# An Lp pooling kernel: all stores from the queue of the loads, in place of a queue of their own

## The chip, the cores and the metric

The kernel runs on one core of a Trainium2 chip. A core has a matrix engine, TensorE (not used here), VectorE (DVE in the profile), ScalarE (ACT), GpSimd (POOL), the SyncE queue (SP) and sixteen DMA engines, which move data between the device memory (HBM, here "dram") and the on-chip memory (SBUF, 128 partitions). A DMA is issued by one of the engines: the profile names the issuing queue SPq or ACTq. The metric is the device time of one execution in microseconds (us). Before the change it is 395.04 us, the median of three runs (394.88 to 395.09).

## The reference

The input is 32 x 256 x 4096 float32, 134.22 MB; the output 32 x 256 x 1024, 33.55 MB. With p = 2 and windows of 4 that don't overlap, each output is the root of the mean of four squares.

```python
batch, channels, length = 32, 256, 4096
kernel_size, p = 4, 2.0
for i in range(length // kernel_size):
    window = np.abs(x[:, :, 4 * i:4 * i + 4]) ** p
    result[:, :, i] = np.mean(window, axis=-1) ** (1.0 / p)
```

Windows lie one after another in memory, so the kernel treats x as one flat row of numbers and cuts it as it likes, in multiples of four.

## The kernel before

The flat input is cut into **groups**. A group's block of x is spread over 128 partitions, so that each partition reads one unbroken run, and its results are one block of the output. Nine groups have two loads each, then one has three and one has one. A load goes into a **slot**; there are three slots' worth of input buffers (52.7 KB per partition each) and two result buffers. The first 18 loads fill a slot each; the last four share two slots.

```python
W, O_W = 13184, 6592
X_SLOTS, O_SLOTS = 3, 2
slots = [[(W, [4416, 4384, 4384])]] * 18
slots += [[(6592, [3296, 3296])] * 2, [(6592, [3296, 3296]), (5056, [2528, 2528])]]
groups = [2] * 9 + [3, 1]
late = {7, 8, 9, 10}     # groups whose results are stored at the very end
in_x = {9, 10}           # groups whose results lie in a free input slot
```

Loads are issued from SP, two slots ahead of the work; the next one is issued as soon as a slot has been summed. Each load is worked in chunks of about 4400 columns: ScalarE squares in place, VectorE sums by fours into the result tile, and ScalarE then takes the root of a quarter of the sum, in place. The root of a chunk is put behind the square of the next chunk, so that ScalarE needn't wait for VectorE.

```python
def load(i):
    ...
    nc.sync.dma_start(out=v, in_=block(xf, g, 1)[:, src:src + w])

stored = {}

def store(g, queue, until=None):
    first = stored.get(g, 0)
    until = columns[g] // k if until is None else until
    queue.dma_start(out=block(of, g, k)[:, first:until], in_=ots[g][:, first:until])
    stored[g] = until

def root(g, o, ends):
    nc.scalar.activation(out=o, in_=o, func=Act.Sqrt, scale=1.0 / k)
    if ends and g not in late:
        store(g, nc.scalar)
    elif g == 0 and g not in stored:
        store(g, nc.scalar, o.shape[1])
...
pending = None
for i in range(n):
    s, _, w, chunks = loads[i]
    while ahead < n and loads[ahead][0] < s + X_SLOTS:
        load(ahead)
        ahead += 1
    ...
    for step in chunks:
        v = xs[i][:, c:c + step]
        nc.scalar.activation(out=v, in_=v, func=Act.Square)
        o = ots[g][:, at + c // k:at + (c + step) // k]
        nc.vector.tensor_reduce(out=o, in_=v.rearrange("p (n j) -> p n j", j=k), ...)
        if pending is not None:
            root(*pending)
        c += step
        pending = (g, o, i == firsts[g] + groups[g] - 1 and c == w)
root(*pending)
for g in sorted(late):
    store(g, nc.sync)
```

Stores go out of two queues. Groups 0 to 6 are stored from the ScalarE queue, right behind the root that ends the group; group 0 in two parts, its first chunk at once and the rest when the group ends. Groups 7 to 10 are stored from SP, after all loads.

Of the kernel before, what the change touches and what calls it, by code (L numbers as in the profile page):

```python
# [1 line left out]

# [4 lines left out]


@with_exitstack
def kernel(  # L10
    ctx: ExitStack,
    tc: tile.TileContext,
    x: bass.AP,
    p: float,
    kernel_size: int,
    out: bass.AP,
):

    nc = tc.nc

    assert float(p) == 2.0, "kernel specialized for p == 2"
    k = int(kernel_size)
    assert k == 4, "kernel specialized for kernel_size == 4"

    P = nc.NUM_PARTITIONS
    fp32 = mybir.dt.float32
    Act = mybir.ActivationFunctionType
    xf = x.rearrange("b c l -> (b c l)")
    of = out.rearrange("b c l -> (b c l)")
    total = xf.shape[0] // P
# [5 lines that stand above are left out]
    groups = [2] * 9 + [3, 1]  # L42
    late = {7, 8, 9, 10}
    in_x = {9, 10}


    loads = [(s, sum(w for w, _ in slot[:j]), *slot[j]) for s, slot in enumerate(slots)
             for j in range(len(slot))]
    n = len(loads)
    assert sum(w for _, _, w, _ in loads) == total  # L50

    firsts = [sum(groups[:g]) for g in range(len(groups))]
    assert sum(groups) == n
    group_of = [g for g, count in enumerate(groups) for _ in range(count)]
    columns = [sum(w for _, _, w, _ in loads[firsts[g]:firsts[g] + groups[g]])
               for g in range(len(groups))]

    x_pool = ctx.enter_context(tc.tile_pool(name="x_pool", bufs=X_SLOTS))
    o_pool = ctx.enter_context(tc.tile_pool(name="o_pool", bufs=O_SLOTS))
    ctx.enter_context(tc.manual_schedule())  # L60

    def block(flat, g, div):
        at, width = sum(columns[:g]) * P // div, columns[g] * P // div
        return flat[at:at + width].rearrange("(p w) -> p w", p=P)

    slot_tiles = {}
    xs = {}

    def load(i):
        s, at, w, _ = loads[i]  # L70
        if at == 0:
            slot_tiles[s] = x_pool.tile([P, W], fp32, name="xt")
        v = slot_tiles[s][:, at:at + w]
        g = group_of[i]
        src = sum(loads[j][2] for j in range(firsts[g], i))
        nc.sync.dma_start(out=v, in_=block(xf, g, 1)[:, src:src + w])  # L76
        xs[i] = v

    ots = {}

    stored = {}

    def store(g, queue, until=None):
        first = stored.get(g, 0)
        until = columns[g] // k if until is None else until
        queue.dma_start(out=block(of, g, k)[:, first:until], in_=ots[g][:, first:until])  # L86
        stored[g] = until

    def root(g, o, ends):
        nc.scalar.activation(out=o, in_=o, func=Act.Sqrt, scale=1.0 / k)  # L90
        if ends and g not in late:
            store(g, nc.scalar)
        elif g == 0 and g not in stored:
            store(g, nc.scalar, o.shape[1])

    ahead = 0
    while ahead < n and loads[ahead][0] < X_SLOTS - 1:
        load(ahead)
        ahead += 1
    pending = None  # L100
    for i in range(n):
        s, _, w, chunks = loads[i]
        while ahead < n and loads[ahead][0] < s + X_SLOTS:
            load(ahead)
            ahead += 1
        g = group_of[i]
        if i == firsts[g]:
            pool, width = (o_pool, O_W) if g not in in_x else (x_pool, W)
            t = pool.tile([P, width], fp32, name="ot" if g not in in_x else "xt")
            ots[g] = t[:, 0:columns[g] // k]  # L110
        at = sum(loads[j][2] for j in range(firsts[g], i)) // k
        assert sum(chunks) == w
        c = 0
        for step in chunks:
            v = xs[i][:, c:c + step]
            nc.scalar.activation(out=v, in_=v, func=Act.Square)  # L116
            o = ots[g][:, at + c // k:at + (c + step) // k]
            nc.vector.tensor_reduce(  # L118
                out=o, in_=v.rearrange("p (n j) -> p n j", j=k),
                axis=mybir.AxisListType.X, op=mybir.AluOpType.add,  # L120
            )
            if pending is not None:
                root(*pending)
            c += step
            pending = (g, o, i == firsts[g] + groups[g] - 1 and c == w)
    root(*pending)
    for g in sorted(late):
        store(g, nc.sync)


# [1 line left out]
_INS = ['x', 'p', 'kernel_size']  # L132
_OUTS = [((32, 256, 1024), 'float32')]

_NUMBERS = {'p': 2.0, 'kernel_size': 4}


# [26 lines left out]
```

## Time and profile before

| | before |
|---|---|
| time, median of 3 | 395.04 us |
| span of the profiled execution | 393.3 us |
| VectorE busy | 282.4 us, 72% |
| ScalarE busy | 292.7 us, 74% |
| bytes moved by DMA | 167.79 MB, mean 427 GB/s |
| a full load (6592 KB), issue to landing | 39.7 us |
| a store of a full group (3296 KB) from the ScalarE queue, issue to landing | 27.1 us |
| square of 4384 columns, ScalarE | 3845 ns |
| sum of 4384 columns by fours, VectorE | 4720 ns |
| root of 1096 columns, ScalarE | 1105 ns |

The profile gives the busy time of each engine, the same in forty equal slices of the span, the DMA queues with their bytes and their share of sixteen engines' time, the chain of work that ended last, and groups of instructions with what they waited for. L90 is the line of the root, L116 that of the square, L118 that of the sum; L76 issues the loads and L86 the stores. In a line such as `[4.84 <-DMA xt<-in_x_dram]` the bracket is the engine's idle time before the instruction, and what ended it. A DMA's time to landing counts from its issue, so it holds the time behind other transfers of its queue as well.

### The profile page before, as it was taken

Reading aid. Unit: us, or ns where it says so; the run is one execution under the profiler, and the core shown is the slowest. Engines: PE = TensorE matmul, PEld = TensorE weight load, DVE = VectorE, ACT = ScalarE, POOL = GpSimd, SP = SyncE. Lnnn points to the kernel's source line nnn. Section 1 sums busy time; section 2 is a strip of 40 time slices with the busy share of each in tenths; the row PEclk is TensorE's granted clock in tenths of the full one; section 3 lists DMA queues with packets and bytes.
Section 4 is the critical chain, followed back from the end, with each engine's and each line's share of the span. In section 5 each row is a group of like instructions: output and inputs, shape, how many; then the busy total and the mean of one; then the engine's idle time right before and its main releaser. Section 6 shows DMA issues by size and latency. Waiting matters only on the chain.

```text
span 393.3 us, 318 instructions
## 1 busy us (share of the span) xinstructions
DVE 282.4 (72%) x62; ACT 292.7 (74%) x126; POOL 0.2 (0%) x4
## 2 busy tenths in 40 slices
DVE  0068979595959495949594959495859586899992
ACT  1098978687776778686868685859595959899991
POOL 0000000000000000000000000000000000000000
DMA  8999998999999999999999999999999999999997
GB/s 343 429 429 447 453 434 366 472 397 434 421 464 424 461 434 400 464 434 430 394 464 426 432 432 432 426 429 442 429 425 434 461 451 429 400 429 428 436 424 304
DMA packets 4898, 167.79 MB, mean 427 GB/s; under 512 B 544, under 2 KB 544, under 8 KB 800
## 3 DMA queue, kind: packets, MB, share of 16 engines
q1 hardware_dynamic: 3744, 144.15, 85.1%
q10 hardware_dynamic: 1152, 23.63, 14.0%
q14 instruction: 2, 0.02, 0.0%
HBM read 134.22 MB, written 33.55 MB: 427 GB/s over the span
## 4 chain that ended last, share of the span: by engine, by line
DMA 58%; ACT 21%; DVE 16%; issue 2%; another core or an unknown queue 1%; ACTq 0%; SPq 0%
DMA xt<-in_x_dram 58%; ACT xt L116 17%; DVE ot L118 12%; DVE xt L118 3%; ACT ot L90 3%; ACT xt L90 1%; ACTq L86 0%; SPq L76 0%; ACTq L116 0%
## 5 line engine op out<-in xcount | busy, mean ns | idle before, releaser
L118 DVE TENSOR_REDUCE ot<-xt 128x1096 f32<-128x4384 f32 (+1 forms) x54 | 255.4, 4731 | 102.9 <-ACT xt L116 102.6
L116 ACT ACTIVATE xt<-xt 128x4384 f32<-128x4384 f32 (+3 forms) x62 | 230.5, 3718 | 89.2 <-DMA xt<-in_x_dram 85.9
L90 ACT ACTIVATE ot<-ot 128x1096 f32<-128x1096 f32 (+1 forms) x54 | 59.9, 1109 | 1.8 <-DVE ot L118 0.9
L118 DVE TENSOR_REDUCE xt<-xt 128x824 f32<-128x3296 f32 (+1 forms) x8 | 27.0, 3385 | 1.3 <-ACT xt L116 1.2
L90 ACT ACTIVATE xt<-xt 128x824 f32<-128x824 f32 (+1 forms) x8 | 6.8, 844 | 3.0 <-DVE xt L118 2.9
L116 ACT ACT_TABLE_LOAD x1 | 1.3, 1283 | 0.7 <-PEq L145 0.7
L90 ACT ACT_TABLE_LOAD x1 | 1.3, 1283 | 0.0
L145 POOL MEMSET const-bfloat16-1.0<- 128x1 bf16 x1 | 0.1, 103 | 0.0
L145 POOL MEMSET const-uint8-127<- 128x1 uint8 x1 | 0.1, 103 | 0.0
L145 POOL MEMSET const-float32-1.0<- 128x1 f32 x1 | 0.1, 100 | 0.0
L145 POOL MEMSET const-float32-0.0<- 128x1 f32 x1 | 0.1, 99 | 0.2 <-issue 0.2
## 6 DMA issues: line engine op xcount, KB each, us to landing
xt<-in_x_dram SPq DMA_DIRECT2D x18, 6592.0 KB, 39.7
out_dram<-ot ACTq DMA_DIRECT2D x6, 3296.0 KB, 27.1
xt<-in_x_dram SPq DMA_DIRECT2D x3, 3296.0 KB, 24.4
out_dram<-ot SPq DMA_DIRECT2D x2, 3296.0 KB, 29.6
out_dram<-ot ACTq DMA_DIRECT2D x1, 2744.0 KB, 27.4
xt<-in_x_dram SPq DMA_DIRECT2D x1, 2528.0 KB, 26.3
out_dram<-xt SPq DMA_DIRECT2D x1, 2472.0 KB, 9.3
out_dram<-xt SPq DMA_DIRECT2D x1, 632.0 KB, 5.0
```

The lines of the kernel that those rows point to most:

```text
L90: nc.scalar.activation(out=o, in_=o, func=Act.Sqrt, scale=1.0 / k)
L116: nc.scalar.activation(out=v, in_=v, func=Act.Square)
L118: nc.vector.tensor_reduce(out=o, in_=v.rearrange("p (n j) -> p n j", j=k), axis=mybir.AxisListType.X, op=mybir.AluOpType.add,)
L145: nc = _bacc.Bacc("TRN2", target_bir_lowering=False, num_devices=1)
```

## The change

All stores are issued from SP, in turn with the loads, and none from ScalarE. The store of a group is still issued where its last root is: behind the first sum of the next group's first load. In SP's order it stands behind the load that was issued ahead for that step, and ahead of the next one. Group 0 is stored in one piece. The aim is one queue in which transfers run in a chosen order, with a ScalarE that issues nothing.

The bookkeeping of pending roots is rewritten as a list, with two numbers, FINE = 0 (from which load on a chunk gets a root of its own) and LAG = 1 (how many chunks later the root comes).

```diff
+    FINE, LAG = 0, 1
...
-    stored = {}
-
-    def store(g, queue, until=None):
-        first = stored.get(g, 0)
-        until = columns[g] // k if until is None else until
-        queue.dma_start(out=block(of, g, k)[:, first:until], in_=ots[g][:, first:until])
-        stored[g] = until
+    def store(g, queue):
+        queue.dma_start(out=block(of, g, k), in_=ots[g])
 
     def root(g, o, ends):
         nc.scalar.activation(out=o, in_=o, func=Act.Sqrt, scale=1.0 / k)
         if ends and g not in late:
-            store(g, nc.scalar)
-        elif g == 0 and g not in stored:
-            store(g, nc.scalar, o.shape[1])
+            store(g, nc.sync)
...
-    pending = None
+    pending = []
+    done = 0
     for i in range(n):
...
-            if pending is not None:
-                root(*pending)
+            total_sum(ots[g][:, summed:summed + step // k], v, i)
+            while pending and pending[0][0] <= done - LAG:
+                root(*pending.pop(0)[1:])
+            done += 1
             c += step
-            pending = (g, o, i == firsts[g] + groups[g] - 1 and c == w)
-    root(*pending)
+            summed += step // k
+            ends = summed == columns[g] // k
+            if ends or i >= FINE:
+                pending.append((done - 1, g, ots[g][:, rooted:summed], ends))
+                rooted = summed
+    for job in pending:
+        root(*job[1:])
     for g in sorted(late):
         store(g, nc.sync)
```

More of the change, by code (lines that the diff above doesn't have):

```diff
@@ L91, in root, with total_sum @@
         if ends and g not in late:
-            store(g, nc.scalar)
-        elif g == 0 and g not in stored:
-            store(g, nc.scalar, o.shape[1])
+            store(g, nc.sync)
+    def total_sum(o, v, i):
+        nc.vector.tensor_reduce(
+            out=o, in_=v.rearrange("p (n j) -> p n j", j=k),
+            axis=mybir.AxisListType.X, op=mybir.AluOpType.add,
+        )
     ahead = 0
@@ L110 @@
             ots[g] = t[:, 0:columns[g] // k]
-        at = sum(loads[j][2] for j in range(firsts[g], i)) // k
+            summed = rooted = 0
         assert sum(chunks) == w
@@ L116 @@
             nc.scalar.activation(out=v, in_=v, func=Act.Square)
[L117 to L121, printed above, removed]
-            if pending is not None:
-                root(*pending)
-            c += step
-            pending = (g, o, i == firsts[g] + groups[g] - 1 and c == w)
-    root(*pending)
+            total_sum(ots[g][:, summed:summed + step // k], v, i)
+            while pending and pending[0][0] <= done - LAG:
+                root(*pending.pop(0)[1:])
+            done += 1
+            c += step
+            summed += step // k
[5 more added lines that the diff above has]
+        root(*job[1:])
     for g in sorted(late):
```

## The prediction
> **What bounds the kernel now.** I read the page first: the DMA row of the forty slices, then the queues, then the chain.
>
> ```profile
> DMA  8999998999999999999999999999999999999997
> q1 hardware_dynamic: 3744, 144.15, 85.1%
> q10 hardware_dynamic: 1152, 23.63, 14.0%
> HBM read 134.22 MB, written 33.55 MB: 427 GB/s over the span
> DMA 58%; ACT 21%; DVE 16%; issue 2%; another core or an unknown queue 1%; ACTq 0%; SPq 0%
> ```
>
> The sixteen DMA engines are never free between the first slice and the last. The shares of the two queues add to 99.1% of sixteen engines' span, so 0.9% of 393.3 us, 3.5 us, is all the DMA time that stands empty, start and end included. Nothing that only moves bytes about can win more than that. The two queues also give a price per byte: q1 (all loads and the last four stores) 144.15 MB in 0.851 x 393.3 = 334.7 us, 430.7 GB/s; q10 (stores alone) 23.63 MB in 0.140 x 393.3 = 55.1 us, 429 GB/s, and that share is rounded by a third of a per cent. A stored byte costs what a loaded byte costs.
>
> Next the beats of the loop, in the timeline of ScalarE: the first square of a slot starts when its load has landed.
>
> ```profile
> 285.43 3.88 ACT L116 ACTIVATE xt<-xt 128x4416 f32<-128x4416 f32 x1 [4.84 <-DMA xt<-in_x_dram]
> 304.93 3.88 ACT L116 ACTIVATE xt<-xt 128x4416 f32<-128x4416 f32 x1 [4.43 <-DMA xt<-in_x_dram]
> 324.34 3.88 ACT L116 ACTIVATE xt<-xt 128x4416 f32<-128x4416 f32 x1 [4.83 <-DMA xt<-in_x_dram]
> 339.98 3.88 ACT L116 ACTIVATE xt<-xt 128x4416 f32<-128x4416 f32 x1 [1.05 <-DMA xt<-in_x_dram]
> ```
>
> A load is 128 x 13184 x 4 B = 6.750 MB, a store of a full group half of it, 3.375 MB. With a store beside them two loads take 324.34 - 285.43 = 38.91 us: 16.875 MB at 433.7 GB/s. The last full load has no store beside it and takes 15.64 us: 431.6 GB/s. Each time ScalarE idles 4.4 to 4.8 us for the load: compute has slack in every slot.
>
> Last, the stretch table, for what the engines do in one such beat, in the unmixed load, and at the end of the kernel where all loads are in and only stores run.
>
> ```profile
> 285.43:324.34 38.91, 28.38 (x6) 29.14 (x12) 0.00 (x0) 1.00 1.00 433
> 324.34:340.00 15.66, 11.52 (x3) 14.54 (x7) 0.00 (x0) 1.00 0.98 426
> 340.00:369.40 29.40, 27.49 (x7) 28.36 (x13) 0.00 (x0) 1.00 1.00 430
> 369.40:377.30 7.90, 7.51 (x4) 7.87 (x6) 0.00 (x0) 1.00 1.02 441
> 377.30:385.10 7.80, 7.34 (x3) 6.46 (x5) 0.00 (x0) 1.00 0.95 411
> ```
>
> Columns are VectorE busy, ScalarE busy, GpSimd, the clock, the DMA share and GB/s. VectorE and ScalarE work 28.4 and 29.1 us of a 38.9 us beat. The GB/s of short stretches swing because a long packet is counted where it falls; landings are surer. The last load is issued at 343.1 us and lands after 26.3 us, at 369.4; the two stores that follow are issued at 343.56 and 359.5 and land after 33.7 and 25.5 us, at 377.3 and 385.0. That is 15.6 us for 6.750 MB, **stores alone** at 432 GB/s, 7.8 us each, out of one queue in which loads went before.
>
> [...] 38.91 us for two loads and a store is what 2 x 15.64 + 7.8 = 39.1 us makes one after the other. [...]
>
> **The change, part by part.** Call the loads L0 to L21, the stores S0 to S10, S6 the last that is not late.
>
> *Removed.* Eight issues of 0.34 us on ScalarE, with some 0.41 us of idle time shown after each. ScalarE has 4.4 to 4.8 us free in every slot, so this is worth 0 on the path. One of eight stores goes (552 KB early, 2744 KB later, become one of 3296 KB): no bytes.
>
> *Unchanged.* The lists with FINE = 0 and LAG = 1 give the old order: each root still follows the square and the sum of the next chunk. All arithmetic and the four late stores stay.
>
> *Moved.* In program order the SP queue is L0 L1 L2 L3 L4 S0 L5 L6 S1 L7 L8 S2 and so on. S(g) waits for a root that ends one square and one root (3.9 + 1.1 us) after a load's landing; the load behind it waits for three sums of that slot, and now SP waits up to 19.1 us for those in any case (309.4 us in 17 waits, by the view of its own waits). So no load is issued later because of the store ahead of it.
>
> *Where the store now runs.* It no longer shares turns with a load but runs whole, after the load issued before it. From the durations above: L0 lands at 19.6, L1 at 35.5, L2 at 51.2, L3 at 66.8, L4 at 82.5, S0 at 90.3, L5 at 106, L6 at 121.6, S1 at 129.4. [...]
>
> *Does the queue stay filled?* L5 needs slot 2: L2 lands at 51.2, plus a square of 3.9 and three sums of 4.73 = 14.2, is 69.4 us; the queue then has work until 90.3. L6 needs slot 0 again: 66.8 + 18.1 = 84.9, with work until 106. Some 21 us are in hand each time.
>
> *The result buffer.* Group g+2 writes into the buffer of group g. S0 lands 7.8 us after L4, the first load of group 2. VectorE could start 3.9 us after that landing and now must wait some 3.9 us more; the same for groups 3 to 8, seven times, 27 us in all. Within the slot: sums from 90.3 to 90.3 + 14.2 = 104.6, and L5 lands only at 106. Slot 1 is free at 104.6, its next load is issued then, and the queue holds work until 129.4. So the wait costs slack and not time.
>
> *The sum.* Landing of L17: 19.57 + 15.94 (L1 as measured) + 16 x 15.64 + 7 x 7.8 = 340.4 us, against 339.98. The tail after it is the same bytes in the same queue and the same chain of squares, sums and roots, 52.4 us to the last landing. **+0.4 us** on 395.04: 395.4.
>
> **The rivals.** *The buffer wait gets on the path.* For it: the wait is real, and the slot that suffers it ends only 1.4 us ahead of the next load. If all 27 us showed, the time would be 422. Against: to delay a load the 21 us in hand in the queue must be used up first, and a beat has 38.9 us for 29.1 of ScalarE work.
>
> *A turn between reading and writing costs time.* The tail shows one change from loads to stores without loss (7.9 us for the first store), but the old trace never shows one queue go from a store back to a load. Seven such joints at 0.3 us each would be 2.1 us: 397.5. Mixed traffic at 433.7 against 431.6 alone leans that way; over the 131.6 MB of L2 to L17 and seven stores the difference is 1.5 us, which gives 396.5.
>
> *One queue is better.* Loads no longer lose turns to stores, so each arrives sooner after its issue. For it: ScalarE is freed. Against: the bytes ahead of L17 are the same, and no more than 3.5 us are empty now, most of it at the start, where L0 takes 19.57 us in place of 15.6. I give it 0.5 us: 394.5.
>
> **Range and chances.** The centre is 395.4 us. The low end, 394.0, is the third rival with a little more than I give it; the high end, 397.6, is the second. 2% is 7.9 us. A gain of that size is more than the empty DMA time, so 0.01. A loss of it needs the buffer wait to empty the queue, or joints of over 1 us each: 0.02. Within 2%: 0.97.
>
> **What would show the steps right or wrong.** Right: DMA shares adding to 98.5% or more, all in q1; two loads and a store still 38.8 to 39.3 us, but uneven, some 15.6 to the group's first load and 23.4 to its second; stores landing some 42 us after issue in place of 27; VectorE waiting for the store of the result, seven times, some 25 to 30 us in all; SP waits for the roots with the loads' own wait shortened by as much. Wrong: an empty stretch in the DMA row at each store, ScalarE's idle time for loads growing by far more than the seven waits, or a load whose time from issue to landing is under 16 us, which would mean that the queue had run dry.

## The result, and the profile after

The changed kernel takes 397.11 us, the median of six runs (396.80 to 397.23); before took 394.92 us in six runs beside them (394.78 to 395.09). The ratio is 1.0055, 95% interval 1.0042 to 1.0068: within 2%, but slower, by 2.2 us at the medians. The spans of the two profiled executions are 395.3 and 393.3 us.

On the page of the changed kernel, the DMA row, the one queue that is left, the chain and the issues of the stores and full loads (in this kernel L85 is the root, L90 the sum and L116 the square):

```profile
DMA  8999999989999999999999999999999999999996
q1 hardware_dynamic: 4752, 167.77, 98.8%
DMA 67%; ACT 15%; DVE 15%; issue 0%; SPq 0%; DVEq 0%; ACTq 0%
xt<-in_x_dram SPq DMA_DIRECT2D x18, 6592.0 KB, 37.4
out_dram<-ot SPq DMA_DIRECT2D x9, 3296.0 KB, 41.8
```

The queue never ran dry: there is no empty slice, the share is 98.8%, and a load has 37.4 us from issue to landing, far above the 15.6 us of its own transfer. A store now waits behind loads and lands after 41.8 us in place of 27.1. In the packets' records of before, the 128 rows of each of S1 to S6 are spread over 20.9 to 21.8 us, with 96 to 98 whole rows of loads in that time; here they lie within 10.4 to 11.3 us, with 14 or 15. The chain holds more DMA than before, 67% for 58%, as it now runs through the stores as well, with 21% of the span.

The view of the waits shows what was moved. First two lines of before, where L90 is the root and L118 the sum, then the changed kernel:

```profile
ACT xt L116 <- DMA xt<-in_x_dram: 85.9, 18, 17.6
ACT ot L90 <- DVE ot L118: 0.9, 1, 0.9
...
DVE ot L90 <- ACT xt L116: 67.0, 29, 23.6
ACT xt L116 <- DMA xt<-in_x_dram: 64.4, 18, 17.7
DVE ot L90 <- DMA out_dram<-ot: 38.7, 7, 6.6
ACT ot L85 <- DVE ot L90: 28.9, 8, 4.0
```

VectorE waits seven times for the result buffer, 38.7 us in all. That is all of its idle time ahead of those seven sums, and some of it is a wait for the load and its square. The first of the seven sums:

```profile
91.51 9.38 DVE L90 TENSOR_REDUCE ot<-xt 128x1104 f32<-128x4416 f32 x2 [6.65 <-DMA out_dram<-ot]
```

Its square ends at 83.68 + 3.88 = 87.56 us (the line is below), so the store alone holds it up for 3.95 us; over the seven it is 27.8 us. ScalarE's wait for loads fell from 85.9 to 64.4 us, and its wait for VectorE rose from 0.9 to 28.9: idle time changed its name.

The loss is in the landings, in ScalarE's timeline. The rows are the first squares of L2, L3, L4, L5, L6, then of L10, L11, L12, and of L17:

```profile
50.85 3.88 ACT L116 ACTIVATE xt<-xt 128x4416 f32<-128x4416 f32 x1 [1.01 <-DMA xt<-in_x_dram]
66.53 3.89 ACT L116 ACTIVATE xt<-xt 128x4416 f32<-128x4416 f32 x1 [1.10 <-DMA xt<-in_x_dram]
83.68 3.88 ACT L116 ACTIVATE xt<-xt 128x4416 f32<-128x4416 f32 x1 [2.57 <-DMA xt<-in_x_dram]
107.00 3.88 ACT L116 ACTIVATE xt<-xt 128x4416 f32<-128x4416 f32 x1 [4.82 <-DMA xt<-in_x_dram]
123.15 3.88 ACT L116 ACTIVATE xt<-xt 128x4416 f32<-128x4416 f32 x1 [1.56 <-DMA xt<-in_x_dram]
...
201.47 3.88 ACT L116 ACTIVATE xt<-xt 128x4416 f32<-128x4416 f32 x1 [0.99 <-DMA xt<-in_x_dram]
224.82 3.88 ACT L116 ACTIVATE xt<-xt 128x4416 f32<-128x4416 f32 x1 [4.83 <-DMA xt<-in_x_dram]
240.40 3.88 ACT L116 ACTIVATE xt<-xt 128x4416 f32<-128x4416 f32 x1 [1.00 <-DMA xt<-in_x_dram]
...
342.07 3.88 ACT L116 ACTIVATE xt<-xt 128x4416 f32<-128x4416 f32 x1 [4.85 <-DMA xt<-in_x_dram]
```

The uneven beat is there: 23.35 us from L10 to L11 (a store lies between) and 15.58 to L12, 38.93 in all, as good as before. But L4, **the load right ahead of the first store**, takes 83.68 - 66.53 = 17.15 us, 1.5 more than L3, and L6, ahead of the second, 16.15. L17 starts at 342.07 us, against 339.98 before. The stretch table has the same by its rate in the last column:

```profile
50.85:66.53 15.68, 14.28 (x4) 14.52 (x6) 0.00 (x0) 1.00 1.00 431
66.53:83.68 17.15, 15.66 (x4) 14.52 (x6) 0.00 (x0) 1.00 1.01 409
83.68:123.15 39.47, 27.30 (x7) 29.03 (x13) 0.00 (x0) 1.00 1.00 431
201.47:240.40 38.93, 28.29 (x7) 29.03 (x12) 0.00 (x0) 1.00 1.00 432
```

409 GB/s at a DMA share of 1.01: the engines are busy all the time, but some packets take longer. The trace keeps every packet. A row, one partition's part of a load, is one packet of 52.7 KB; it takes an engine 1.947 us at the median in both kernels, a row of a full store 0.978 us. Below, from the packets' own records, are the times by which packets after 22 us were over the median of their size (those over by more than 0.05 us), summed over the sixteen engines; the part of them between 95 us and the end of L17, without the two rows in each run that stand beside a fetch of instructions; and the times at which engines ended, by their own landings:

```
            late time   first cluster of late packets   late time    L4 and S0 in,   L17, first    L17, last
            engine-us   (us of the span: engine-us)     after 95 us  last engine     engine ends   engine ends
before        12.8      30-51: 2.9;  59-65: 8.5             0.0         90.79          338.28        339.89
after         25.6      78-80: 16.6                         7.4         91.39          338.64        341.99
all_act       14.4      43-50: 2.0;  54-61: 11.4            0.1         89.93          338.30        339.52
s0_only_sp    17.9      78-79: 15.2                         1.0         90.42          338.29        339.85
s0_act        27.4      57-63: 18.8                         7.6         90.48          338.63        340.82
early_sp      19.9      47-49: 15.0                         4.0         91.38          338.38        341.42
twice         34.8      76-79: 17.1                        13.3         91.06          339.06        342.19
turns14       25.7      76-79: 18.4                         4.1           -            339.61        342.33
cut_before    25.3      78-81: 18.1                         5.7         91.11          338.90        341.59
no_inline      1.0      none                                0.0           -            283.17        284.34
```

(All but the first two are experiments, below; each line is one profiled execution.) In the changed kernel all sixteen engines are late at 78 to 80 us, about 1.0 us each, with their last row of L4, the one right ahead of S0 (one engine with the row before it too). Small clusters of 0.9 to 2.6 engine-us lie at 119, 157, 236, 275 and 315 us, one ahead of each of S1, S2, S4, S5 and S6, on four to ten engines each. At L17 the quickest engine is only 0.36 us later than before, and the slowest 2.1 us. ScalarE starts on L17 at 342.07 us, behind the slowest engine, so that is the loss.

In these two executions the first store is the lesser part of it. When L4 and S0 are both in, the slowest engine is 0.6 us behind before (91.39 against 90.79); the other 1.5 us come over the six later stores. Before has late packets at its first store too, 11.4 engine-us in its two parts. What it has none of is late time after 95 us.

### The profile page after: what moved, and what is told of

Same layout as the page of the kernel before. It is cut to its first block, busy times and chain, and to the rows that moved or that the text cites. A ratio compares the mean times of both kernels' runs of the same rounds, so it can differ in the third digit from the quotient of the medians.

```text
span 395.3 us, 330 instructions
## 1 busy us (share of the span) xinstructions
DVE 281.7 (71%) x62; ACT 291.8 (74%) x126; POOL 0.2 (0%) x4
## 3 DMA queue, kind: packets, MB, share of 16 engines
q1 hardware_dynamic: 4752, 167.77, 98.8%
## 4 chain that ended last, share of the span: by engine, by line
DMA 67%; ACT 15%; DVE 15%; issue 0%; SPq 0%; DVEq 0%; ACTq 0%
DMA xt<-in_x_dram 46%; DMA out_dram<-ot 21%; ACT xt L116 12%; DVE ot L90 12%; DVE xt L90 3%; ACT ot L85 2%; ACT xt L85 1%; SPq L76 0%; DVEq L90 0%; ACTq L116 0%
## 5 line engine op out<-in xcount | busy, mean ns | idle before, releaser
L90 DVE TENSOR_REDUCE ot<-xt 128x1096 f32<-128x4384 f32 (+1 forms) x54 | 254.7, 4729 | 105.7 <-ACT xt L116 67.0
L116 ACT ACTIVATE xt<-xt 128x4384 f32<-128x4384 f32 (+3 forms) x62 | 230.3, 3716 | 64.4 <-DMA xt<-in_x_dram 64.4
L85 ACT ACTIVATE ot<-ot 128x1096 f32<-128x1096 f32 (+1 forms) x54 | 59.9, 1110 | 29.6 <-DVE ot L90 28.9
L90 DVE TENSOR_REDUCE xt<-xt 128x824 f32<-128x3296 f32 (+1 forms) x8 | 27.0, 3384 | 1.3 <-ACT xt L116 1.2
L85 ACT ACTIVATE xt<-xt 128x824 f32<-128x824 f32 (+1 forms) x8 | 6.7, 843 | 3.0 <-DVE xt L90 2.9
## 6 DMA issues: line engine op xcount, KB each, us to landing
xt<-in_x_dram SPq DMA_DIRECT2D x18, 6592.0 KB, 37.4
out_dram<-ot SPq DMA_DIRECT2D x9, 3296.0 KB, 41.8
```

## The experiments

A **ring** here means the row of transfers of one queue. Theory **J**: a joint from a load to a store in one ring delays the load's last packets. Rivals: **E**, the early store of the first chunk was what before gained from; **B**, VectorE's wait for the result buffer costs the time. P and F, later, divide J.

**all_act**: the stores go back to ScalarE's queue, but whole.

```diff
         if ends and g not in late:
-            store(g, nc.sync)
+            store(g, nc.scalar)
```

> The changed kernel with the seven inline stores, each whole, on the ScalarE queue: against before it lacks only the early store of the first chunk. Theory J (each joint from a load to a store in one ring costs time on some DMA engines, and none joins when the stores have a ring of their own): 394.9 to 395.4 us, last waits of VectorE for a store gone. Theory E (the early first chunk of before was what saved the time): 396.5 us or more. Theory B (VectorE's wait for the result buffer is what costs): as J, 395, since a shared turn lands the store early.

Measured: 394.73 us against 394.79 of before, a ratio of 0.9999 (0.9991 to 1.0008), 0.2 us under J's figure. E falls: the early part of group 0 is worth nothing, and the rewritten lists cost nothing. The queue is the whole change.

**s0_only_sp** and **s0_act**: the first store on one queue, the other six on the other.

```diff
-            store(g, nc.sync)
+            store(g, nc.sync if g == 0 else nc.scalar)     # s0_only_sp
+            store(g, nc.scalar if g == 0 else nc.sync)     # s0_act
```

> S0 alone on the SP queue, S1 to S6 on the ScalarE queue. Theory J with a dear first joint (in the changed kernel's trace all sixteen DMA engines are about 1 us late there, against about 0.45 us in the trace of before): 395.3 to 395.9 us, that is about 0.4 to 0.8 of the 2.2 us. Theory J with equal joints, and theory B (one of seven waits): 395.2 us, a seventh of 2.2 us above before.

> S0 on the ScalarE queue, S1 to S6 on SP. Theory J with a dear first joint: 396.3 to 396.7 us. Equal joints, or theory B: 396.8 us, six sevenths of 2.2 us above before.

Measured: 396.01 us for S0 alone on SP, 1.0028 of before (1.0021 to 1.0035), and 396.57 us for the six others, 1.0043 (1.0029 to 1.0057), against 394.79 of before. By the times, S0 alone brings 1.2 us, more than J with a dear first joint gave it, and the six others 1.8; the interval of the six holds the figures of both forms of J. That the two add to 3.0 and not to 2.2 is not explained.

The traces do not bear out a dear first joint in the ring. In s0_act the first store in the ring of the loads is S1, and no row ahead of it is late. The sixteen engines are late at S0 instead, 18.8 engine-us, though S0 has the ScalarE queue to itself. In these runs, what makes all the engines late goes with the first store of the kernel, in whichever queue. Its size varies: all_act does the same work in the same queues up to S1 and has 13.4 engine-us there. And in s0_only_sp the profiled execution, the quickest of a wide scatter (394.97 to 396.50), has the late rows at S0, 15.2 engine-us, with L4 at 16.69 us, and is still as quick as before; what made the others slower is in no trace.

The later stores set the runs apart. With S1 to S6 on the ScalarE queue (before, all_act, s0_only_sp) there are 0.0 to 1.0 engine-us of late time after 95 us, and the slowest engine takes 249.1 to 249.6 us from the landing of L4 and S0 to that of L17. With S1 to S6 among the loads (after, s0_act, early_sp, twice) it is 4.0 to 13.3 engine-us and 250.0 to 251.1 us.

**early_sp**: group 0 in two parts as before, both on SP.

```diff
         if ends and g not in late:
             store(g, nc.sync)
+        elif g == 0 and g not in stored:
+            store(g, nc.sync, o.shape[1])
```

> The changed kernel with group 0 stored in two parts as before, first chunk early, both on SP. Theory E (the early part saves time by itself): 396.2 us or less. Theory J: one joint more, 397.1 to 397.5 us, unless the first joint's cost is one of first use and is shared out, then 396.9 us.

Measured: 396.94 us, 1.0054 (1.0041 to 1.0066), the same as the changed kernel. The timeline of ScalarE says more: the first squares of L1 to L4 (here the square is L123).

```profile
35.20 3.88 ACT L123 ACTIVATE xt<-xt 128x4416 f32<-128x4416 f32 x1 [0.75 <-DMA xt<-in_x_dram]
52.31 3.88 ACT L123 ACTIVATE xt<-xt 128x4416 f32<-128x4416 f32 x1 [2.53 <-DMA xt<-in_x_dram]
69.34 3.88 ACT L123 ACTIVATE xt<-xt 128x4416 f32<-128x4416 f32 x1 [2.45 <-DMA xt<-in_x_dram]
84.91 3.88 ACT L123 ACTIVATE xt<-xt 128x4416 f32<-128x4416 f32 x1 [1.00 <-DMA xt<-in_x_dram]
```

The early part now stands behind L2, and L2 is the load that takes 17.11 us. (L3 takes 17.03, of which 1.3 us is the part's own 0.565 MB, an estimate at the 430.7 GB/s of q1 in before.) L4, ahead of the rest of S0, takes 15.57: no delay. The delay of all the engines moves with the kernel's first store, and in this run it comes once, though that store is small.

**no_inline**: S0 to S6 are left out, so the results of groups 0 to 6 are not written.

```diff
-        if ends and g not in late:
-            store(g, nc.sync)
```

> The changed kernel without its seven inline stores: groups 0 to 6 are worked but not stored, so seven joints and 23.6 MB are left out. A store's packets alone take seven times 7.83 us, 54.8 us, in the trace of the changed kernel. Theory J: the joints' cost of about 2 us goes as well, 340.0 to 340.6 us, with the sixteen engines of a load landing within 1.3 to 1.7 us of each other to the end. If the loss is a slower pace of loads over time, not tied to stores: 342.3 us.

Measured: 339.69 us, 0.8602 of before (0.8590 to 0.8613), 0.3 us below J's figure; a slower pace of the loads, not tied to stores, falls. Loads L14 to L17 in ScalarE's timeline (here the square is L114):

```profile
237.59 3.88 ACT L114 ACTIVATE xt<-xt 128x4416 f32<-128x4416 f32 x1 [1.00 <-DMA xt<-in_x_dram]
253.18 3.88 ACT L114 ACTIVATE xt<-xt 128x4416 f32<-128x4416 f32 x1 [1.01 <-DMA xt<-in_x_dram]
268.83 3.88 ACT L114 ACTIVATE xt<-xt 128x4416 f32<-128x4416 f32 x1 [1.08 <-DMA xt<-in_x_dram]
284.43 3.88 ACT L114 ACTIVATE xt<-xt 128x4416 f32<-128x4416 f32 x1 [1.01 <-DMA xt<-in_x_dram]
```

A load alone takes 15.6 us to the end, and only the two rows beside the fetches of instructions are late. Seven stores are 7 x 7.83 = 54.8 us of packets (eight rows of 0.978 us on each engine), so by this estimate 394.5 us would be a kernel whose stores cost their packets alone. Before pays 0.4 us above that for having stores, and the changed kernel 2.6. The first store here is the late S7, which stands behind L21 and has no load behind it; no packet was late there.

**twice**: the first sum of groups 2 to 8 is done a second time, right behind VectorE's wait for the buffer.

```diff
             total_sum(ots[g][:, summed:summed + step // k], v, i)
+            if 2 <= g <= 8 and i == firsts[g] and c == 0:
+                total_sum(ots[g][:, summed:summed + step // k], v, i)
```

> The changed kernel with the first sum of groups 2 to 8 done twice (the same result again): VectorE's work behind the wait for the result buffer grows by 4.7 us in seven slots, 33 us in all, so its end in such a slot comes 10 us late in place of 5.5. Theory J: 397.0 to 397.4 us, slack takes it. Theory B (the wait for the buffer costs the 2.2 us): over 399 us, as each slot has lost what slack it had.

Measured: 396.97 us, 1.0053 (1.0040 to 1.0067), the same as without. The waits:

```profile
ACT ot L85 <- DVE ot L90: 63.3, 8, 9.2
DVE ot L90 <- DMA out_dram<-ot: 39.0, 7, 6.7
DVE ot L90 <- ACT xt L116: 33.1, 27, 23.2
ACT xt L116 <- DMA xt<-in_x_dram: 30.3, 12, 17.3
```

33 us of added VectorE work came out of ScalarE's wait for loads (64.4 to 30.3 us) and not out of the time. The buffer wait is slack, with 4.7 us more to spare in each such slot. B falls.

**turns14** and **turns7**: stores in two halves, the load behind in two pieces; in turns14 they alternate, in turns7 not.

```diff
+    # in load(i), for the load behind a store: a first piece of 4416 columns, then the rest
+        nc.sync.dma_start(out=v[:, 0:cut], in_=block(xf, g, 1)[:, src:src + cut])
+        second(rest.pop())        # turns14: the store's second half comes here
         nc.sync.dma_start(out=v[:, cut:w], in_=block(xf, g, 1)[:, src + cut:src + w])
...
-            store(g, nc.sync)
+            # first half of the columns here; in turns7 the second right behind it
```

> Each inline store cut into two halves by columns, and the load behind it into pieces of 4416 and 8768 columns, in the order store half, load piece, store half, rest of the load: fourteen joints from load to store with the same bytes. Theory J with equal joints: 2 us over its twin with seven joints. Theory J where the first joint is the dear one: 0.5 to 1.5 us over the twin. Theory B: the store's second half lands some 5 us later, no change if that is slack.

> The twin of the last: the same cuts, in the order store half, store half, load piece, rest of the load, so seven joints. All theories: 397 to 397.5 us, the changed kernel with some more packets.

Measured: 397.48 us (1.0065, 1.0052 to 1.0077) and 397.43 us (1.0065, 1.0052 to 1.0079). Seven more joints cost nothing that shows, so J with equal joints falls. So does J with a dear first joint in the form it had here, which gave the added ones 0.5 us or more. The loss does not go by the number of joints. VectorE's wait for stores grew to 74.4 us in turns14 and was again slack. The late time is still 25.7 engine-us, 18.4 of it at the first joint.

**cut_before, cut_behind, half_store, cut_half**: does the length of the packets at the joint matter?

```diff
+        cut = 8800 if i in range(4, 17, 2) else 0      # cut_before, cut_half: ahead of a store
+        cut = 8800 if i in range(5, 18, 2) else 0      # cut_behind: behind a store
+        if cut:
+            nc.sync.dma_start(out=v[:, 0:cut], in_=block(xf, g, 1)[:, src:src + cut])
+        nc.sync.dma_start(out=v[:, cut:w], in_=block(xf, g, 1)[:, src + cut:src + w])
...
+        half = columns[g] // k // 2 if g < 7 else 0    # half_store, cut_half: two stores, by columns
```

> The changed kernel, where each load that stands right ahead of an inline store (L4, L6 to L16) is cut into pieces of 8800 and 4384 columns, so that the packets right ahead of the store are 17.5 KB and not 52.7 KB. Theory P (a long load packet is held up by the store's packets that are begun behind it, and the loss goes with the packet's length; the run without inline stores, whose first store stands behind 20 KB packets, showed no delay there): no late packets at the joints, engines within 1.8 us at the end, 395.2 to 396.0 us with the price of 56 more packets on each engine counted (about 9 ns each, 0.5 us, from the runs with halves). Theory F (the first store of a kernel costs its 0.9 us whatever stands ahead, and the others are chance): 397.2 to 397.6 us.

> The control: the same cut in the loads right behind an inline store (L5, L7 to L17), the packets ahead of the stores stay long. Both theories: 397.3 to 397.8 us, the changed kernel and 0.5 us for more packets.

> The changed kernel with each inline store cut into two halves by columns, one behind the other, loads uncut: packets of 13 KB in the store, of 52.7 KB ahead of it. If the store's packet length sets the loss at S1 to S6 (as the few late packets of the runs with halves suggest): 397.0 us, 0.5 us more for packets and 0.6 us less at the slowest engine. If only the load's packet counts: 397.5 us.

> Both: loads ahead of a store cut, stores in halves. Theory P: the joints are free, 395.6 to 396.2 us, of which 1 us is the price of 112 more packets on each engine. Theory F: 397.5 us and more.

Measured: 396.88, 396.84, 397.18 and 397.41 us, ratios 1.0056 (1.0042 to 1.0070), 1.0058 (1.0045 to 1.0071), 1.0061 (1.0048 to 1.0073) and 1.0069 (1.0056 to 1.0081). P falls: with 17.5 KB rows ahead of S0, two of an engine's eight were late, the sixth and the seventh, 18.1 engine-us, as much as one long row. F fits the first store, but is a name and no mechanism, and that the other late packets are chance does not fit their absence where S1 to S6 have a queue of their own; its figures were 0.3 us too high in cut_before, and cut_behind fell below what both theories gave it, as the price of more packets was too high an estimate. None of the four is clearly apart from the changed kernel's 397.11, and none beats before.

**What stays open.** That the queue of the stores makes the 2.2 us is shown, and that they are the lag of the slowest engine. Why is not. At the kernel's first store rows on all the engines were late, in either queue (16.6 engine-us in the changed kernel, 18.8 in s0_act), and in no_inline none was; but there it had no loads behind it, came 230 us later and stood behind shorter rows (20.2 KB for 52.7). The small clusters ahead of later stores were there only where those stores stood among the loads (4.0 to 13.3 engine-us after 95 us, against 0.0 to 1.0). They were seen and counted, in one trace of each run, and not explained.

## Why the prediction was right, and where its sum was off

- **Bound by DMA, no gain to be had:** right. The shares of 99.1% and 98.8% and the 394.5 us worked out from no_inline leave, by that estimate, some 0.4 us for any order of transfers. The slack of 4.4 to 4.8 us "in every slot" was read off slots with a store beside them; the fourth line of that view, of the load without one, has 1.05.
- **ScalarE's issues are worth 0:** right; all_act has seven of them and takes 394.73 us against 394.79 of before. But there was more to the second queue than the time of issuing: with it the stores had a ring of their own, and that was worth 2.2 us (394.92 against 397.11).
- **The queue stays filled:** right; 37.4 us from issue to landing, and twice took 33 us more of VectorE work without a longer time.
- **The buffer wait is slack:** right, and in size too: 27 us were forecast, and 27.8 of the 38.7 us lie behind the end of the square.
- **The sum, + 0.4 us, was the term that failed.** It put the landing of L17 at 340.4 us; it came at 342.0. Two errors lie in it. A load alone was taken as 15.64 us and is 15.59, which made the sum 0.8 us too high over sixteen loads. And the seven stores stood in it at their packets alone. With the measured sizes (L0 in at 19.67, L1 15.57 us later, then 16 x 15.59 + 7 x 7.83) the sum is 339.5 us, so what was left out is 2.5 us, by which the slowest engine is behind its packets. Before has some 0.4 us of the same, and the difference is the 2.1 us. The rival that priced the joints at 2.1 us, 397.5, came true within 0.4 us, and set the upper end of the range. That its size fits is luck: the 0.3 us a joint was the author's guess, which no trace shows, and the picture was another, seven equal turns from a store back to a load, where the late packets are those of the load ahead of the store and seven more joints cost nothing.
- **The rival of one better queue** has nothing for it: loads landed no sooner at the end (L17 at 341.99 us against 339.89), and no variant with a store among the loads of SP was as quick as before by its median.
- **The reading that misled:** one joint in the tail, at S7, was taken to show that turns from loads to stores are free. It was true of that joint (7.9 us for S7, with 7.8 for a store alone), which is not the kernel's first store and has no loads behind it.

## What to carry to other kernels

When the DMA share is as high as here (99.1%) and the compute engines have slack, work out the time of the packets alone and see how much is left above it: here, by the estimate from no_inline, 0.4 us of 394.9, a tenth of a per cent, was all that a change of queue could win. In this case stores were cheaper in a ring of their own (some 0.4 us above their packets, by the same estimate) than in turn with the loads (2.6 us), and ScalarE's 0.34 us per DMA cost nothing (394.73 us in all_act), since it had idle time (85.9 us of waits for loads in before). The work on L17 began with the slowest engine: the first of the sixteen had ended at 338.64 us, the last at 341.99, and the square started at 342.07. So when a stretch is slow at full DMA share, look at how long the packets take, and when the last engine ends.

## What the runs showed of the hardware that was not expected

- Packets are very even, 1.947 us for 52.7 KB of a load, with 95% at or below 1.956 us; but ahead of the first store of the changed kernel the last such row on each of the sixteen engines took 2.6 to 3.3 us. In s0_act, where that store had a queue of its own, the engines were late too (18.8 engine-us, against 16.6).
- In the one ring of the changed kernel the engines' lag stays. The spread between the first and the last engine's end of a load grows in the changed kernel from 1.3 us (L0 to L3) to 3.3 us (L17) and is not made up by then; in no_inline it is 1.1 to 1.2 us throughout.
- Two fetches of instructions (8 KB on queue 14) in before, at 179 and 291 us, each stood beside a load packet that took 0.3 and 0.6 us longer than the rest, on one engine. The other traces have two such fetches among the loads as well, with rows late by 0.25 to 0.38 and by 0.57 to 0.66 us.
